# The zeroth MLP group's Relus pinned in ScalarE's order, and its sum operands spaced further apart

## The chip, the cores and the metric

The kernel runs on one core of one Trainium2 chip. The metric is the device time of one execution in microseconds (us). TensorE is named PE in the profile, VectorE DVE, ScalarE ACT, GpSimd POOL and SyncE SP.

## The reference

A hybrid decoder layer on 512 tokens of width 2048: attention heads and a recurrence side by side, then an MLP with a squared Relu. Only the MLP's entry matters here.

```python
h = rmsnorm(x, g_norm_mlp[l]).astype(jnp.float32) * (1.0 + sc2) + sh2
hid = jnp.square(jax.nn.relu(jnp.einsum('bsd,df->bsf', h, w_mlp_in[l].astype(jnp.float32))))
y = jnp.einsum('bsf,fd->bsd', hid, w_mlp_out[l].astype(jnp.float32))
x = (x.astype(jnp.float32) + gt2 * y).astype(x.dtype)
...
return rmsnorm(x, g_norm_final)
```

`w_mlp_in` is 2048 x 8192, `w_mlp_out` 8192 x 2048, all in float32.

## The kernel before

Every float32 operand of a matmul is split into a high part (a rounding copy on ScalarE) and a low part (the difference, on VectorE), and a product is three matmuls: high by high, high by low and low by high. `split` (L124) does it for activations, with its two instructions at L126 and, through `low`, at L122; `operands` (L1053) does it for weights. L122 is thus the line of all low parts, whatever their tile.

The 8192 hidden columns are done in 16 groups of 512. The tokens are cut in two halves of 256, A and B.

The zeroth group (g = 0) is a plain product, `half_product` (L991), in 16 steps of k for half A and 16 for half B (lines 259, 262 and 263 on PE, weight copies at L244). Each half writes two banks of PSUM: A a `z` and an `mm`, B an `o` and an `mm`. There are eight banks: three `z`, four `mm` and one `o`. `relu_half` (L977) empties a half's two banks with two Relus on ScalarE (L981). `keep_parts` (L928) then squares them, splits them and writes parts and sums to DRAM through POOL's queue (lines 932 to 949).

Groups 1 to 15 are products after Strassen and Winograd, in `strassen` (L1083): per group eight steps j, in each step seven products of two halves and three matmuls (lines 1102 to 1104), which is 42 matmuls of 256 columns. The seven products sum up in seven banks, taken in turn; group 1 has `z` `z` `z` `mm` `mm` `mm` `mm`, group 2 begins with `o`. Group 1 takes j from 7 down to 0, the others from 0 up. For each step `operands` loads 512 KB of weights on SP's queue (L1058), forms the weight sums on VectorE (lines 1060, 1067, 1068), and splits raw weights (a ScalarE copy of 768 columns at L1066, into tiles `w3`) and sums (one of 1024 columns at L1072, into tiles `w4`/`w5`). There are six `w3` tiles and five of 1024 columns, and one set takes two of each.

The activation sums are made once, in `sums` (L907): for each j from 7 to 0, four VectorE operations of 256 columns (L912 to L915), and two splits of 512 columns each (L126, L122). Group 1 needs the sums of j at its step j.

The order on each engine is fixed before the run. A scheduler walks a modelled time line, and on each engine takes the ready instruction with the highest priority. Priority is the place in program order; `tc.high_priority(offset=n)` moves the enclosed instructions n places forward. `tc.keep_in_program_order(ins)` adds an order-only edge: on its engine `ins` comes behind the instruction that was traced just before it. SETW (200) is the offset of the operands, SETE (330) that of what empties the banks at a group's end.

Work beside the products is traced by generators in lanes (`bg`). After each step `tick()` takes 1.0 off the lane's wait, and while the wait is not above zero the lane's next piece is traced; a piece yields the wait that it adds. `norm3`, `prep_b` and `sums` are queued before half A, `keep_parts(0)` after half B. By these numbers `sums` traces j = 7 at the third step of half B (16 steps), 6 at the sixth, 5 at the ninth, 4 at the twelfth, and 3, 2, 1, 0 at the 13th to 16th. `acts_in` (L1123) makes sure that a j is traced before its use.

Of the kernel before, what the change touches and what calls it, by code (L numbers as in the profile page):

```python
# [12 lines left out]
AF = mybir.ActivationFunctionType  # L13
# [51 lines left out]
def hybrid_layer_kernel(  # L65
# [32 lines left out]
    def T(tag, dt=F32, cols=None):  # L98
        return new(next(split_tag) if tag == "w4" else tag, dt, cols)
# [13 lines left out]
    act = nc.scalar.activation  # L113
# [7 lines left out]
    def low(out, full, high):  # L121
        tt(out=out, in0=full, in1=f32(high), op=ALU.subtract)  # L122

    def split(full, tag):  # L124
        h = T(tag, F32R)
        act(h, full, AF.Copy)  # L126
        lo = T(tag, F32R)
        low(lo, full, h)
        return h, lo
# [311 lines left out]
    for o in range(8):  # L441
        t = T("a")
# [275 lines left out]
    def mix(k, src, gcol, r):  # L718
        stt(out=src, in0=src, scalar=gcol, in1=r, op0=ALU.mult, op1=ALU.mult)
        mixed[k] = split(src, "a")  # L720
# [138 lines left out]

    KP = NK // 2
    NG = DFF // 512
    HT = 256
# [2 lines left out]
    raw_h, raw_l, fin, fin2, half2, other, sums_ = {}, {}, {}, {}, {}, {}, {}  # L867
# [10 lines left out]
    def prep_a(r2):  # L878

        for k in PAIRED:  # L880
            j, c = k % KP, k // KP
            if c == 0:
# [9 lines left out]
    def prep_b(r2):  # L892

        for k in BACK:
            j, c = k % KP, k // KP
            if c == 0:
# [10 lines left out]
    def sums():  # L907

        for j in range(KP)[::-1]:
            f1, f2 = fin[j], fin2[j]  # L910
            s12, s34 = T("n"), T("n")
            tt(out=s12[:, q_(0)], in0=f2[:, q_(0)], in1=f2[:, q_(1)], op=ALU.subtract)  # L912
            tt(out=s34[:, q_(0)], in0=f1[:, q_(0)], in1=f2[:, q_(0)], op=ALU.subtract)
            tt(out=s12[:, q_(1)], in0=s12[:, q_(0)], in1=f1[:, q_(0)], op=ALU.subtract)
            tt(out=s34[:, q_(1)], in0=f1[:, q_(1)], in1=s12[:, q_(1)], op=ALU.add)  # L915
            sums_[j] = [split(t, "a") for t in (s12, s34)]
            yield 3.0 if j > 4 else 1.0

    def norm3(tok, prep, ptag):
        yield 5.0  # L920
# [7 lines left out]
    def keep_parts(g, r11, r12, r22, r21, dt=1.0):  # L928

        for n, r in enumerate((r11, r12, r22, r21)):  # L930
            if g:
                act(r, r, AF.Relu)
            act(r, r, AF.Square)
            if n < 3 or p21D[g]:
                for i, t in enumerate(split(r, "a")):
                    dst = (
                        partD[g].rearrange("p (b f i t) -> p b f i t", b=2, f=3, i=2)[:, :, n, i, :] if n < 3
                        else p21D[g].rearrange("p (b i t) -> p b i t", b=2, i=2)[:, :, i, :]
                    )
                    nc.gpsimd.dma_start(dst, f32(t).rearrange("p (b t) -> p b t", b=2))  # L940
            yield dt
        dst = sumD[g].rearrange("p (b n t) -> p b n t", b=2, n=4)
        s1, s2 = T("a"), T("a")
        for n, (out, i0, i1, op) in enumerate((
            (s1, r21, r22, ALU.subtract), (s2, s1, r11, ALU.subtract), (r11, r11, r21, ALU.subtract),
            (r12, r12, s2, ALU.add),
        )):
            tt(out=out, in0=i0, in1=i1, op=op)
            nc.gpsimd.dma_start(dst[:, :, n, :], out.rearrange("p (b t) -> p b t", b=2))
            yield dt  # L950
# [26 lines left out]
    def relu_half(bs):  # L977

        rs = T("a"), T("a")
        for r, b in zip(rs, bs):  # L980
            act(r, b, AF.Relu)  # L981
        return rs


    PAIRED = [k for j in range(KP) for k in (j, j + KP)]
    BACK = [k for j in range(KP)[::-1] for k in (j, j + KP)]

# [20 lines left out]
    def h2_half(tok):  # L1008
        def of(k):
            j, c = k % KP, k // KP  # L1010
            if tok.start == 0:
                return raw_h[j][:, q_(c)], raw_l[j][:, q_(c)]
            side = half2 if c else other
            while j not in side:
                assert bg.next()
            return side[j][:, q_(0)], side[j][:, q_(1)]
# [22 lines left out]
    for k in range(12, NK):  # L1039
        nc.gpsimd.dma_start(x1D[k], x1[k])  # L1040
    b2 = [bank("z"), bank("mm")]
    bg.add(norm3(B, prep_b, "z"), sums())
    held = {}
    half_product(b2, in_src(0), h2_half(A), PAIRED, held, dict(zip(PAIRED[6:], ["w3"] * 3 + ["ts"] * 2 + ["w4"] * 5)))
    r11, r12 = relu_half(b2)
    b2 = [bank("o"), bank("mm")]
    half_product(b2, in_src(0), h2_half(B), BACK, held)
    r21, r22 = relu_half(b2)
    bg.add(keep_parts(0, r11, r12, r22, r21, 0.7))

    SETW, SETE = 200, 330

    def operands(src):  # L1053

# [28 lines left out]
    def strassen(src, acts, after=None, pre=None, before=None, js=range(8)):  # L1083

        bs = [bank(next(turn)) for _ in PRODUCTS]
        if pre:
            n, ts = pre
            with tc.high_priority(offset=SETE):
                for b, t in zip(bs, ts):
                    act(b, t, AF.Copy)  # L1090
                for b, t in zip(bs[5:], load_pre(n, (5, 6), nc.scalar)):
                    act(b, t, AF.Copy)
        if before:
            loaded[0] = before()
        for j in js:
            w, a = operands(src(j)), acts(j)
            for b, (an, wn) in zip(bs, PRODUCTS):
                (ah, al), (wh, wl) = a[an], w[wn]
                for i in range(2):
                    out, st = b[:, q_(i)], j == js[0] and i == 0 and not pre  # L1100
                    kw = dict(skip_group_check=True)
                    mm(out, wh[:, blk(i)], ah, start=st, stop=False, **kw)  # L1102
                    mm(out, wh[:, blk(i)], al, start=False, stop=False, **kw)  # L1103
                    mm(out, wl[:, blk(i)], ah, start=False, stop=j == js[-1], **kw)  # L1104
            if after:
                after(j)
            tick()
        return bs
# [108 lines left out]
    for g in range(1, NG):  # L1217
# [3 lines left out]
        bs = strassen(lambda j: w_pair[j][:, :, g * 512 : (g + 1) * 512], acts_in, last, js=range(KP)[:: -1 if g == 1 else 1])  # L1221
        with tc.high_priority(offset=SETE):
            r = [T("a") for _ in range(4)]
            q11, q12, q22, q21 = combine(bs, *r)

            rs = q12, q11, q21, q22
# [30 lines left out]
    for i, (n, ps) in enumerate(parts):  # L1257
# [15 lines left out]
        bs = strassen(src, acts_out, after, nxt, before, ps)  # L1273
        nxt = loaded[0]
        if n not in left:
# [11 lines left out]
            with tc.high_priority(offset=SETW):  # L1287
                for k, tok, q in quarters(n, *qs):
                    t = x2[k][:, tok]
# [5 lines left out]
        else:  # L1295
            with tc.high_priority(offset=SETE):
                for j, b in enumerate(bs):
                    t = T("a")
# [14 lines left out]
    for p in final:  # L1313
        t = T("a", F32R)
# [51 lines left out]
    def part(o, i):  # L1366

        if o == 0 and i == 3:
            for k in range(11, NK):
                sums(A, k)  # L1370
            bg.add(norm4(A))
        if o > 0 and i == 3:
            sums(B, 10 + o)
# [95 lines left out]
```

## Time and profile before

| | us |
|---|---|
| median of 3 runs | 1995.27 |
| lowest, highest run | 1991.86, 1996.58 |
| the profiled execution | 1994.49 |
| its span in the profile | 1992.7 |
| PE busy | 1941.9 |
| DVE busy | 1760.6 |
| ACT busy | 1074.6 |
| POOL busy | 193.6 |

The rows shown below are of the profiled execution; their first number is the start in us from the beginning of the span, the second the duration. In brackets stands how long the engine was idle before the instruction, and what ended that. A PE row's duration is modelled and overlaps the next; the distance of starts tells the pace. DVE and ACT rows overlap a little too.

### The profile page before, as it was taken

What the parts mean: (1) busy time and instruction counts of PE and PEld (TensorE: products, weight loads), DVE (VectorE), ACT (ScalarE), POOL (GpSimd) and SP (SyncE); (2) the same over time, 40 slices, a digit from 0 to 9 for tenths busy, and PEclk for the clock granted to TensorE, in tenths of its full rate; (3) what the DMA queues carried; (4) which work ended last, traced back from release to release, by engine and by line L of the source; (5) the groups of instructions that cost most, each with busy time, mean ns of one, the idle gap of its engine ahead of it and who ended that gap; (6) DMA issues with size and microseconds to landing.
All of it is one profiled execution on the core that took longest, in us unless ns stands there. A gap on an engine that the chain in (4) does not pass through costs nothing. (4 is left out here: it accounts for less than half of the span.)

```text
span 1992.7 us, 37203 instructions
## 1 busy us (share of the span) xinstructions
PE 1941.9 (97%) x14148; PEld 1815.3 (91%) x14148; DVE 1760.6 (88%) x2979; ACT 1074.6 (54%) x1580; POOL 193.6 (10%) x307
## 2 busy tenths in 40 slices
PE   8999999999999998999999999999999999999997
PEld 6787887788888998999999999999999999999996
DVE  8998776988998599999999999999879779879996
ACT  5443564786433385555555555556445555556552
POOL 0000000000000000112111211200110210211100
PEclk9999999999999999999999999999999999999998
DMA  9896655556779544766666665755567668679653
GB/s 368 304 340 198 212 163 185 179 163 218 226 251 365 170 134 129 239 194 213 221 196 203 226 197 190 232 173 210 185 241 262 238 249 278 220 253 341 225 197 112
DMA packets 205238, 443.51 MB, mean 223 GB/s; under 512 B 20481, under 2 KB 42113, under 8 KB 205058
## 3 DMA queue, kind: packets, MB, share of 16 engines
q1 hardware_dynamic: 176338, 356.58, 54.2%
q0 software_dynamic: 23680, 77.61, 10.5%
q10 hardware_dynamic: 5040, 6.93, 1.0%
q8 instruction: 111, 1.82, 0.4%
q14 instruction: 69, 0.57, 0.1%
HBM read 376.30 MB, written 64.75 MB: 221 GB/s over the span
## 5 line engine op out<-in xcount | busy, mean ns | idle before, releaser
L1102 PE MATMUL ps_mm<-a,w 128*128 128x256 f32 x1696 | 469.1, 277 | 3.0 <-DVE a L1114 1.2
L1104 PE MATMUL ps_mm<-a,w 128*128 128x256 f32 x1696 | 469.2, 277 | 0.4 <-DVE w L122 0.3
L1103 PE MATMUL ps_mm<-a,w 128*128 128x256 f32 x1696 | 469.1, 277 | 0.4 <-DVE a L122 0.3
L1072 ACT ACTIVATE w<-ts 128x1024 fp32r<-128x1024 f32 x244 | 258.4, 1059 | 273.1 <-DVE ts L1068 241.5
L1104 PE MATMUL ps_z<-a,w 128*128 128x256 f32 x1304 | 362.0, 278 | 6.9 <-DVE w L122 6.8
L1102 PE MATMUL ps_z<-a,w 128*128 128x256 f32 x1304 | 362.2, 278 | 3.4 <-DVE a L1118 1.6
L1103 PE MATMUL ps_z<-a,w 128*128 128x256 f32 x1304 | 361.4, 277 | 0.1
L122 DVE TENSOR_TENSOR w<-ts,w 128x1024 fp32r<-128x1024 f32 x244 | 297.8, 1221 | 55.4 <-PE ps_mm L1103 20.4
L1102 PEld LDWEIGHTS ps_mm<-a,w 128*128 128x128 f32 x1696 | 318.4, 188 | 4.3 <-issue 2.5
L1104 PEld LDWEIGHTS ps_mm<-a,w 128*128 128x128 f32 x1696 | 318.7, 188 | 1.1 <-DVE w L122 1.0
L1103 PEld LDWEIGHTS ps_mm<-a,w 128*128 128x128 f32 x1696 | 318.7, 188 | 0.8 <-DVE a L122 0.8
L122 DVE TENSOR_TENSOR w<-raw,w 128x768 fp32r<-128x768 f32 (+1 forms) x296 | 267.5, 905 | 37.8 <-ACT w L244 24.0
L1066 ACT ACTIVATE w<-raw 128x768 fp32r<-128x768 f32 x244 | 204.5, 839 | 174.8 <-issue 80.5
L1104 PEld LDWEIGHTS ps_z<-a,w 128*128 128x128 f32 x1304 | 245.6, 189 | 8.2 <-DVE w L122 8.1
L1102 PEld LDWEIGHTS ps_z<-a,w 128*128 128x128 f32 x1304 | 245.8, 188 | 4.9 <-issue 2.1
L1103 PEld LDWEIGHTS ps_z<-a,w 128*128 128x128 f32 x1304 | 245.7, 188 | 0.6 <-DVE a L122 0.6
L244 ACT ACTIVATE wh<-wr 128x512 fp32r<-128x512 f32 (+1 forms) x184 | 113.2, 618 | 142.4 <-PE ps_mm L262 61.8
L1060 DVE TENSOR_TENSOR ts<-raw 128x512 f32<-128x512 f32 x244 | 166.8, 684 | 14.2 <-DMA raw<-in_w_mlp_out_dram 13.4
L259 PE MATMUL ps_mm<-a,wh 128*128 128x512 f32 x448 | 176.8, 395 | 2.6 <-DVE a L460 1.0
L263 PE MATMUL ps_mm<-a,wl 128*128 128x512 f32 x448 | 175.0, 391 | 1.5 <-DVE wl L122 1.3
L262 PE MATMUL ps_mm<-a,wh 128*128 128x512 f32 x448 | 174.9, 390 | 0.0
L211 DVE SCALAR_TENSOR_TENSOR x<-x,cb 128x1024 f32<-128x1024 f32 x108 | 131.2, 1218 | 23.4 <-DMA x<-in_w_adaT_dram 23.3
(336 smaller groups left out, 4007.7 us busy)
## 6 DMA issues: line engine op xcount, KB each, us to landing
raw<-in_w_mlp_out_dram SPq DMA_DIRECT2D x124, 512.0 KB, 4.6
raw<-in_w_mlp_in_dram SPq DMA_DIRECT2D x120, 512.0 KB, 3.8
x<-in_w_adaT_dram SPq DMA_DIRECT2D x108, 512.0 KB, 5.6
wr<-in_w_in_dram SPq DMA_DIRECT2D x160, 256.0 KB, 3.4
tt<-in_w_adaT_dram SPq DMA_DIRECT2D x52, 512.0 KB, 6.2
part<-a POOLq DMA_DIRECT2D x84, 256.0 KB, 3.9
a<-part SPq DMA_DIRECT2D x84, 256.0 KB, 6.3
prod<-a POOLq DMA_DIRECT2D x63, 256.0 KB, 5.8
```

The costliest lines, as they stand in the source:

```text
L122: tt(out=out, in0=full, in1=f32(high), op=ALU.subtract)
L211: ins = stt(out=t, in0=t, scalar=1.0, in1=cb[q_], op0=ALU.mult, op1=ALU.mult, accum_out=self.ga[:, q_ : q_ + 1],)
L244: act(h[:, :n], r[:, :n], AF.Copy)
L259: first = mm(out, wh, ah, start=start, stop=False, **kw)
L262: mm(out, wh, al, start=False, stop=False, **kw)
L263: mm(out, wl, ah, start=False, stop=stop, **kw)
L1060: tt(out=t[:, : 2 * HT].rearrange("p (a b) -> p a b", a=2), in0=r[:, HT : 3 * HT].rearrange("p (a b) -> p a b", a=2), in1=r[:, q_(0)].unsq ...
L1066: act(h, r[:, HT:], AF.Copy)
L1072: act(h, t, AF.Copy)
L1102: mm(out, wh[:, blk(i)], ah, start=st, stop=False, **kw)
L1103: mm(out, wh[:, blk(i)], al, start=False, stop=False, **kw)
L1104: mm(out, wl[:, blk(i)], ah, start=False, stop=j == js[-1], **kw)
```

## The change

`sums` yields 3.0 for j above 3 (before: above 4), 2.0 for j of 3 and 2, and 1.0 for 1 and 0. By the ticks, j = 7 to 4 stay in their steps of half B, 3 goes to the 15th, and 2, 1 and 0 are traced after the first, third and fourth step of group 1. The ScalarE copies of the splits for j = 2, 1, 0 are pinned behind the ScalarE instruction traced just before each. The Relus of both halves get priority SETE and the same pin, and the `mm` bank comes first in each pair. SETW and SETE are defined earlier, with the same values.

```diff
-    def split(full, tag):
+    def split(full, tag, late=False):
         h = T(tag, F32R)
-        act(h, full, AF.Copy)
+        ins = act(h, full, AF.Copy)
+        if late:
+            tc.keep_in_program_order(ins)
         lo = T(tag, F32R)
         low(lo, full, h)
         return h, lo
...
+    SETW, SETE = 200, 330
...
-            sums_[j] = [split(t, "a") for t in (s12, s34)]
-            yield 3.0 if j > 4 else 1.0
+            sums_[j] = [split(t, "a", late=j < 3) for t in (s12, s34)]
+            yield 3.0 if j > 3 else 2.0 if j > 1 else 1.0
...
     def relu_half(bs):
 
         rs = T("a"), T("a")
-        for r, b in zip(rs, bs):
-            act(r, b, AF.Relu)
+        with tc.high_priority(offset=SETE):
+            for r, b in reversed(list(zip(rs, bs))):
+                tc.keep_in_program_order(act(r, b, AF.Relu))
         return rs
...
-    SETW, SETE = 200, 330
-
     def operands(src):
```

## The prediction

> **What bounds the kernel now.** I read the page's totals first, then a table of busy time by stage, then the waits of that stage, then the instructions in order of time on TensorE, ScalarE and VectorE.
>
> ```profile
> PE 1941.9 (97%) x14148; PEld 1815.3 (91%) x14148; DVE 1760.6 (88%) x2979; ACT 1074.6 (54%) x1580; POOL 193.6 (10%) x307
> ```
>
> TensorE is the bound on average, so time can come only from places where it does not run. The table shows such a place where the MLP begins (columns: busy us of PE, PEld, DVE, ACT, POOL, granted clock, DMA share, GB/s).
>
> ```profile
> 768.00:781.00 13.00, 7.21 (x55) 6.82 (x54) 13.00 (x28) 7.89 (x14) 0.00 (x0) 0.87 0.20 63
> 781.00:793.00 12.00, 12.00 (x93) 11.98 (x91) 8.91 (x14) 5.70 (x10) 2.88 (x5) 0.86 0.27 81
> ...
> 754.00:805.00 51.00, 44.23 (x351) 43.03 (x351) 47.03 (x83) 27.13 (x40) 5.42 (x8) 0.93 0.48 158
> 805.00:843.00 38.00, 37.29 (x325) 36.89 (x324) 36.89 (x60) 21.91 (x29) 6.80 (x10) 1.00 0.67 205
> ...
> 1400.00:1500.00 100.00, 100.00 (x885) 100.00 (x884) 80.64 (x122) 47.20 (x58) 10.22 (x19) 1.00 0.64 223
> ```
>
> From 768 to 781 us VectorE is busy all the time and TensorE only 7.21 of 13 us; just after it, VectorE has room (8.91 of 12). So work for VectorE is bunched. A matmul costs 100 us / 885 = 0.113 us where nothing disturbs (1400 to 1500). Of the waits between 754 and 805 us (total, times, longest) this one carries TensorE's loss:
>
> ```profile
> PE ps_z L1104 <- DVE w L122: 6.2, 4, 4.2
> ```
>
> TensorE waits for a low half of weights from VectorE. In order of time:
>
> ```profile
> 758.89 0.28 PE L1102 MATMUL ps_z<-a,w 128*128 128x256 f32 x1
> ...
> 770.72 0.28 PE L1103 MATMUL ps_z<-a,w 128*128 128x256 f32 x1
> 772.61 0.39 PE L1104 MATMUL ps_z<-a,w 128*128 128x256 f32 x1 [1.61 <-DVE w L122]
> 772.83 0.28 PE L1102 MATMUL ps_z<-a,w 128*128 128x256 f32 x1
> 772.95 0.28 PE L1103 MATMUL ps_z<-a,w 128*128 128x256 f32 x1
> ...
> 779.58 0.58 PE L1104 MATMUL ps_z<-a,w 128*128 128x256 f32 x1 [4.18 <-DVE w L122]
> 779.96 0.42 PE L1102 MATMUL ps_z<-a,w 128*128 128x256 f32 x1
> 780.17 0.42 PE L1103 MATMUL ps_z<-a,w 128*128 128x256 f32 x1
> ...
> 784.43 0.28 PE L1103 MATMUL ps_z<-a,w 128*128 128x256 f32 x1
> 784.55 0.28 PE L1104 MATMUL ps_z<-a,w 128*128 128x256 f32 x1
> 784.67 0.28 PE L1102 MATMUL ps_mm<-a,w 128*128 128x256 f32 x1
> ...
> 807.53 0.28 PE L1102 MATMUL ps_o<-a,w 128*128 128x256 f32 x1
> ```
>
> Group 1 runs from 758.89, right behind the zeroth group's second half, to 807.53, where group 2 opens with its bank `o`: 48.64 us. It has 8 x 7 x 6 = 336 matmuls, at 0.113 that is 38.0 us. So 10.6 us are lost here. Two terms are large: the 4.18 us wait, and the stretch behind it, 779.96 to 784.43, where starts lie 0.21 apart instead of 0.113: 4.47 us of which 4.47 x (1 - 0.113/0.21) = 2.1 are loss.
>
> Why does it wait? ScalarE:
>
> ```profile
> 742.38 0.51 ACT L902 ACTIVATE a<-n,mods 128x256 f32<-128x256 f32 x1
> 742.78 0.59 ACT L981 ACTIVATE a<-ps_z 128x512 f32<-128x512 f32 x1
> ...
> 755.20 0.61 ACT L244 ACTIVATE w<-raw 128x512 fp32r<-128x512 f32 x1
> ...
> 757.07 1.06 ACT L1072 ACTIVATE w<-ts 128x1024 fp32r<-128x1024 f32 x1 [0.52 <-DVE ts L1068]
> ...
> 760.87 0.85 ACT L1066 ACTIVATE w<-raw 128x768 fp32r<-128x768 f32 x1 [2.74 <-DMA raw<-in_w_mlp_in_dram]
> ...
> 764.90 1.06 ACT L1072 ACTIVATE w<-ts 128x1024 fp32r<-128x1024 f32 x1 [1.71 <-DVE ts L1068]
> ...
> 780.48 0.57 ACT L981 ACTIVATE a<-ps_o 128x512 f32<-128x512 f32 x1
> 780.96 0.58 ACT L981 ACTIVATE a<-ps_mm 128x512 f32<-128x512 f32 x1
> ...
> 786.35 1.06 ACT L1072 ACTIVATE w<-ts 128x1024 fp32r<-128x1024 f32 x1 [3.77 <-PE ps_mm L1104]
> ```
>
> Half B's two Relus (L981, the last pair) have their input at about 759.1 (the last matmul of half B starts just before 758.89 and runs 0.28) and run at 780.5 and 781.0. Nothing but their place in ScalarE's queue holds them: it idles 2.74 us right then. Until then the second one's bank `mm` is full, and it is the fourth `mm` bank that group 1 needs for its seventh product. So that product's matmuls of j = 7 to 4 come only from 784.67 on, and the weight tiles they read stay taken: each operand set takes two of the five 1024-column tiles, so the third set (copied at 764.90) finds no tile for its low half.
>
> VectorE shows that, and gives the prices:
>
> ```profile
> 754.39 0.69 DVE L1060 TENSOR_TENSOR ts<-raw 128x512 f32<-128x512 f32 x1 [0.69 <-DMA raw<-in_w_mlp_in_dram]
> ...
> 757.48 0.69 DVE L1060 TENSOR_TENSOR ts<-raw 128x512 f32<-128x512 f32 x1
> 758.08 0.95 DVE L122 TENSOR_TENSOR w<-raw,w 128x768 fp32r<-128x768 f32 x1
> 758.95 1.22 DVE L122 TENSOR_TENSOR w<-ts,w 128x1024 fp32r<-128x1024 f32 x1
> 760.08 0.42 DVE L1067 TENSOR_TENSOR ts<-ts,raw 128x256 f32<-128x256 f32 x1
> 760.42 0.69 DVE L122 TENSOR_TENSOR a<-n,a 128x512 fp32r<-128x512 f32 x1
> 761.02 0.42 DVE L1068 TENSOR_TENSOR ts<-ts,raw 128x256 f32<-128x256 f32 x1
> 761.36 0.69 DVE L1060 TENSOR_TENSOR ts<-raw 128x512 f32<-128x512 f32 x1
> ...
> 786.23 2.43 DVE L122 TENSOR_TENSOR w<-ts,w 128x1024 fp32r<-128x1024 f32 x2 [2.83 <-PE ps_mm L1103]
> ...
> 800.44 1.22 DVE L122 TENSOR_TENSOR w<-ts,w 128x1024 fp32r<-128x1024 f32 x1
> ```
>
> That low half is written at 786.23, after 2.83 us of waiting for the seventh product; the circle is closed there. Start to start, an operand set costs 0.60 + 0.87 + 1.13 + 0.34 + 0.34 = 3.28 us of VectorE, and one j of the sums four 256-column operations and two 512-column low halves, 4 x 0.34 + 2 x 0.60 = 2.56.
>
> **The change part by part.** No instruction, DMA or byte is added or removed; orders change.
>
> Relus of half A: the pin puts them behind the prep copies traced before them. They run right behind one already (742.38, 742.78), without a gap: 0.
>
> Relus of half B, the `mm` bank first, priority raised: the pin's last predecessor is the weight copy at 755.20 (L244). They can go when TensorE ends half B, at 759.1, into the 2.74 us gap before 760.87; two take about 1.05 (780.48 to 781.43 is 0.48 each, start to start). The seventh product of j = 7 is due 36 matmuls behind 758.89, at 763.0, so it finds its bank, and the low half of the third set no longer waits for 786.
>
> Spacing: j = 7, 6, 5, 4 of the sums keep their steps, j = 3 comes three steps behind j = 4 instead of one, at the 15th of half B's 16 steps; j = 2, 1, 0 land behind the first, third and fourth steps of group 1, each before its use (sixth, seventh, eighth). So their VectorE work, 2.56 each, no longer stands in front of the fourth operand set. Queue order for the split copies of these three: behind the 1024-column copies of j = 7, 5 and 4. At j = 7 and 5 that was so already (copies at 757.07 and 764.90, sums later); for j = 0 it is new, and costs nothing if that copy comes by 780, since its sum is used last.
>
> How far can group 1 shrink? VectorE is then the limit. From 754.39 it owes: 8 operand sets, 26.2; sums of j = 3 to 0, 10.2; what is left of j = 5 and 4, about 1.5 and 2.2; one weight low half, 0.6. Sum 40.8, so it could be through at 795.2. In the profile its last operand of group 1 (800.44) ends at 801.7: the difference is the 2.83, small handshakes, and some 2.7 us of the zeroth group's own splits and of group 2's operands in between. Behind its last operand TensorE needs at least four products of six matmuls, 2.7 us; in the profile it took 807.5 - 801.7 = 5.8.
> - Best end: 795.2 + 2.7 = 797.9, a gain of 9.6 us. (TensorE's own floor is 758.9 + 38.0 = 796.9.)
> - Poor end: 795.2 + 3.3 (handshakes and foreign work) + 5.8 = 804.3, a gain of 3.2.
> - I take the middle, 6.4, since order is set by costs that I cannot see.
>
> In both ends the remaining waits are spread over eight steps of at most 2.6 us each, so I leave out the slow stretch. The nearest rows: behind the 1.61 us wait the starts are 0.12 apart, behind the 4.18 us wait 0.21. The Trainium skill, page "TensorE: Matmul & The Clock Gate", section "What's actually happening", says that the clock falls to one half after an idle window of about 3.4 us and comes back after as long a busy one. Both rows agree with it; by its figure the slow stretch would cost about 1.7 us where the trace has 2.1.
>
> What is late next: the zeroth group's parts (L933, L126, L948) start four to five steps later in program order. Before, three splits and two sums of it, 5 x 0.60 = 3.0 us of VectorE, ran inside group 1. They now fall on group 2, where VectorE has 1.1 us free in 38. They feed only DMAs of POOL's queue that are read back much later, so they may slide on; bounds 0 and 3.0. I take 0.5, near the low end, since no operand set waits behind them by priority. SP's loads of raw weights move forward with the buffers; the DMA share there is 0.48, so they have room: 0.
>
> Sum: 6.4 - 0.5 = 5.9 us. The profiled execution took 1994.49 (span 1992.7 and 1.8 around it), 0.8 less than the median of 1995.27; from the median the forecast is 1989.4, and behind group 1 nothing else is forecast to move.
>
> **The rivals.**
> - VectorE's time is conserved. It is 92% busy from 754 to 805 and 97% in group 2, so pushed-off work may come back as waits later. Then only its 2.83 us wait is won: 1995.3 - 2.8 = 1992.5. For it: the 36.89 of 38. Against: TensorE runs 37.29 of those 38 us.
> - The pinned Relu blocks ScalarE. If it is placed right behind the copy at 755.20, it stands at about 755.7 and waits for 759.1; the copies of j = 6 and j = 7 behind it come 3.4 us later, and VectorE with them: 1989.4 + 3.4 = 1992.8. Against: it is issued only when the schedule holds its bank for complete. The Trainium skill, same page, section "Architectural detail", calls ScalarE's queue a strict FIFO; the 3.77 us in which ScalarE runs nothing ahead of the waiting copy at 786.35 agree.
> - The Relus do not move, and the order stays about as it is: 1995.3. Against: the idle gap above.
> - Slower: the late sums become what TensorE waits for. The place is the split copies of j = 2, 1, 0, pinned behind the 1024-column copies; if one of these waits for a weight tile as at 786.35 (3.77 us), the split and the low half on VectorE wait too. Three such waits are 11.3 us, with one slow stretch 13.4. It decides, that is it costs 4 us net, once they reach 5.9 + 4.0 = 9.9: 1995.3 - 5.9 + 13.4 = 2002.8. For it: five tiles for two per set. Against: the late use.
>
> **How the numbers follow.** 0.2% is 4.0 us, about what a measurement of this kernel can tell. The forecast (gain 3.2 to 9.6, less 0.5) has 0.72, of which 0.67 beyond 4.0; conserved time 0.12, same; blocked ScalarE 0.06, half faster, half same; no move 0.05, same; late sums 0.05, slower. Faster 0.70, same 0.25, slower 0.05. The forecast's own range is 1985.7 to 1992.5; with the two cases at 1992.5 and 1992.8 and their spread of some 1.5 the range is 1985.3 to 1994.2.
>
> **What would show it.** Right: L981 of banks `mm` and `o` near 760 instead of 780; group 1's seventh product in turn; no wait of L1104 over 3.4 us; granted clock 1.00 from 768 to 793; first `ps_o` of group 2 near 801; VectorE's wait at 783 gone. Wrong: L1102 or L1103 waiting for `a` of L122, ScalarE idle before L981, or group 2 and 3 longer than before by what group 1 won.

## The result, and the profile after

The change made the kernel slower: a median of 1999.68 us in 11 runs against 1995.27 us in 11 runs of the kernel before, ratio 1.0023 (95% interval 1.0014 to 1.0032). Forecast were 1989.4 us, a range that ended at 1994.2, and a chance of 0.05 for slower.

The profiled execution that came with these runs was a disturbed one of 6918.82 us in which the matmuls were slow; such executions count in the medians of this document but not in its ratios, which so need not be the quotients of the medians. The profile after is therefore read from the run `again`, which has the same instructions in the same order on each engine and the line numbers of the kernel before. That execution took 2000.34 us, with a span of 1998.6; before had a span of 1992.7.

First the table of busy time by stage, of `again`, for the stretches shown of before and the ones behind them (busy us of PE, PEld, DVE, ACT, POOL, granted clock, DMA share, GB/s):

```profile
768.00:781.00 13.00, 9.28 (x67) 9.08 (x67) 12.99 (x26) 8.53 (x14) 0.00 (x0) 0.87 0.14 42
781.00:793.00 12.00, 12.00 (x108) 12.00 (x107) 11.17 (x19) 5.75 (x8) 0.00 (x0) 1.00 0.44 132
...
806.00:820.00 14.00, 9.16 (x64) 8.92 (x64) 10.86 (x18) 5.80 (x9) 3.38 (x5) 0.76 0.59 218
754.00:805.00 51.00, 46.23 (x384) 45.30 (x382) 49.35 (x89) 28.71 (x41) 2.74 (x4) 0.97 0.47 145
805.00:843.00 38.00, 32.68 (x269) 32.22 (x269) 33.81 (x58) 19.25 (x26) 10.17 (x15) 0.91 0.69 232
```

The reader compares the last two rows with those of before. From 754 to 805 us 384 matmuls run where 351 ran: the aimed-at place did gain. From 805 to 843 us only 269 run where 325 ran: a new hole, and the row of 806 to 820 us shows where it is, with TensorE busy 9.16 of 14 us and a granted clock of 0.76. Before, little was lost there:

```profile
806.00:820.00 14.00, 13.29 (x114) 12.89 (x114) 13.96 (x22) 9.59 (x15) 2.03 (x3) 1.00 0.51 157
```

TensorE's waits between 754 and 850 us in `again` (total, times, longest) name both places:

```profile
PE ps_mm L1102 <- ACT a L981: 3.7, 1, 3.7
PE ps_z L1102 <- ACT a L1113: 3.7, 1, 3.7
PE ps_o L1104 <- DVE w L122: 1.1, 1, 1.1
```

The waits of L1104 behind L122, weights' low halves, that led this list before (6.8 us in this window, 6.2 of them up to 805 us) have shrunk to 1.4 (1.1 at `ps_o`, 0.3 at `ps_z`). In their place TensorE waits once for a Relu of half B (L981), and once for L1113, the ScalarE copy that begins the combination of group 1's banks and so frees the first bank for group 2. ScalarE in order of time:

```profile
766.37 0.63 ACT L126 ACTIVATE a<-n 128x512 fp32r<-128x512 f32 x1 [0.47 <-DVE n L914]
...
771.06 1.30 ACT L126 ACTIVATE a<-n 128x512 fp32r<-128x512 f32 x2 [2.38 <-DVE n L914]
772.26 0.83 ACT L1066 ACTIVATE w<-raw 128x768 fp32r<-128x768 f32 x1
773.00 0.58 ACT L981 ACTIVATE a<-ps_mm 128x512 f32<-128x512 f32 x1
773.47 0.59 ACT L981 ACTIVATE a<-ps_o 128x512 f32<-128x512 f32 x1
...
804.13 0.63 ACT L126 ACTIVATE a<-a 128x512 fp32r<-128x512 f32 x1 [2.44 <-DMA part<-a]
804.67 0.83 ACT L1066 ACTIVATE w<-raw 128x768 fp32r<-128x768 f32 x1
805.41 1.04 ACT L1072 ACTIVATE w<-ts 128x1024 fp32r<-128x1024 f32 x1
810.96 0.60 ACT L1113 ACTIVATE a<-ps_z 128x512 f32<-128x512 f32 x1 [4.51 <-DMA part<-a]
```

Two things are to be seen. The Relus came forward from 780.5 to 773.0, not to 759: sum copies (L126) that wait for VectorE still stand ahead of them. And the copy L1113, which ran at 804.49 before, runs at 810.96, because its *output* tile is still being read by a DMA that writes a part of the zeroth group to DRAM (`part<-a`); ScalarE idles 4.51 us for that, and 2.44 us for another tile just before. In the kernel before the copy does not wait:

```profile
804.49 0.57 ACT L1113 ACTIVATE a<-ps_z 128x512 f32<-128x512 f32 x1
```

POOL's queue shows how late these DMAs are issued, first in `again`:

```profile
799.62 0.70 POOL L940 DMA_DIRECT2D part<-a  x1 [85.00 <-ACT a L126]
...
808.67 0.68 POOL L940 DMA_DIRECT2D part<-a  x1 [2.94 <-DVE a L122]
```

and then in the kernel before:

```profile
782.35 0.70 POOL L940 DMA_DIRECT2D part<-a  x1 [67.79 <-ACT a L126]
...
794.19 0.68 POOL L940 DMA_DIRECT2D part<-a  x1 [0.67 <-DVE a L122]
```

The zeroth group's six parts went out between 782 and 794 us, well ahead of group 1's combination; now they go out between 800 and 809 us, across it. TensorE in `again`:

```profile
773.62 0.39 PE L1102 MATMUL ps_mm<-a,w 128*128 128x256 f32 x1 [3.73 <-ACT a L981]
...
774.33 0.41 PE L1103 MATMUL ps_mm<-a,w 128*128 128x256 f32 x1
774.54 0.41 PE L1104 MATMUL ps_mm<-a,w 128*128 128x256 f32 x1
...
803.54 0.28 PE L1102 MATMUL ps_o<-a,w 128*128 128x256 f32 x1
...
811.61 0.58 PE L1102 MATMUL ps_z<-a,w 128*128 128x256 f32 x1 [3.72 <-ACT a L1113]
811.99 0.41 PE L1103 MATMUL ps_z<-a,w 128*128 128x256 f32 x1
812.21 0.41 PE L1104 MATMUL ps_z<-a,w 128*128 128x256 f32 x1
```

Group 2 opens at 803.54 (807.53 before). Eighteen matmuls later it needs the `z` bank, waits 3.72 us, and then runs at 0.21 us from start to start, half pace, as it did behind the 3.73 us wait at 773.62. The Trainium skill, page "TensorE: Matmul & The Clock Gate", section "What's actually happening", gives an idle window of about 3.4 us for the fall to half clock; both rows agree.

The fixed order on TensorE has changed as well. In the kernel before, only six `ps_o` matmuls of group 2 stand ahead of its first `ps_z` one:

```profile
808.21 0.28 PE L1102 MATMUL ps_z<-a,w 128*128 128x256 f32 x1
```

In `again` it is eighteen, those of three steps, so TensorE comes sooner to the operands of the later steps and waits for them, 0.48 us at 805.55 and 1.12 us at 807.17. An estimate from these rows: the three waits of this stage make 5.3 us, and from 811.61 to 814.98 fifteen matmuls take 3.4 us where 15 x 0.113 = 1.7 would do; less the one wait of 0.64 us that the kernel before has in this stage, that is 6.4 us.

Four marks cut the span into stages: the first matmul of group 1, the first `ps_o` of group 2, and the L1113 of groups 2 and 15. All profiled executions, in us:

| kernel | group 1 to `ps_o` | `ps_o` to combination of 2 | 2 to 15 | 15 to the end | first part issued |
|---|---|---|---|---|---|
| before | 48.6 | 37.7 | 507.4 | 640.1 | 782.4 |
| before_again | 48.0 | 37.8 | 505.7 | 640.1 | |
| again (the change) | 44.4 | 44.3 | 505.7 | 645.0 | 799.6 |
| again_2 (the change) | 45.1 | 44.5 | 506.8 | 644.4 | |
| relus | 47.8 | 38.6 | 509.9 | 641.7 | |
| sums | 45.6 | 44.0 | 505.0 | 646.6 | |
| c_in_n | 44.3 | 43.9 | 506.2 | 644.2 | |
| parts_late | 45.9 | 44.7 | 505.6 | 644.6 | 786.0 |
| parts_early | 42.5 | 38.4 | 509.8 | 643.2 | 780.2 |
| parts_early_2 | 43.8 | 38.5 | 507.2 | 641.7 | |
| early_parts | 42.0 | 41.7 | 505.4 | 643.1 | |
| early4_parts | 43.4 | 41.3 | 509.1 | 641.0 | |
| lane_alone | 48.5 | 39.2 | 506.5 | 640.1 | 782.6 |

From before to `again`: -4.2, +6.6, -1.7, +4.9 and +0.3 ahead of group 1, together +5.9, the difference of the two spans. So there are two losses to explain, one in group 2 and one behind group 15, and a gain that is smaller than forecast.

The mark at the first `ps_o` is the end of group 1 only where all 336 matmuls of group 1 run ahead of it. That is so in the first eight rows and in `lane_alone`. In `parts_early` and `parts_early_2` 22 of them run behind it, in `early_parts` and `early4_parts` 24. Counted by matmuls, 336 have begun after 45.1, 46.6, 48.3 and 47.9 us in these four, against 48.6 and 48.0 in the two executions of the kernel before.

### The profile page after: what moved, and what is told of

Read it like the earlier page. It is cut to its first block, busy times and chain, and to the rows that moved or that the text cites. A ratio compares the mean times of both kernels' runs of the same rounds, so it can differ in the third digit from the quotient of the medians.

```text
span 6917.1 us, 37211 instructions
## 1 busy us (share of the span) xinstructions
PE 6898.7 (100%) x14148; PEld 5852.2 (85%) x14148; DVE 1799.5 (26%) x2979; ACT 1105.9 (16%) x1580; POOL 192.7 (3%) x307
## 4 chain that ended last, share of the span: by engine, by line
PE 100%; DVE 0%; ACT 0%; DMA 0%; issue 0%; DVEq 0%
PE ps_mm L1105 10%; PE ps_mm L1104 10%; PE ps_mm L1106 10%; PE ps_z L1105 8%; PE ps_z L1106 8%; PE ps_z L1104 8%; PE ps_mm L261 7%; PE ps_mm L264 7%; PE ps_mm L265 7%; PE ps_z L261 3%; PE ps_z L264 3%; PE ps_z L265 3%; PE ps_o L1105 3%; PE ps_o L1104 2%; PE ps_o L1106 2%; PE ps_o L264 1%
## 5 line engine op out<-in xcount | busy, mean ns | idle before, releaser
L1105 PE MATMUL ps_mm<-a,w 128*128 128x256 f32 x1696 | 1176.4, 694 | 0.0
L1106 PE MATMUL ps_mm<-a,w 128*128 128x256 f32 x1696 | 1151.6, 679 | 0.0
L1104 PE MATMUL ps_mm<-a,w 128*128 128x256 f32 x1696 | 1151.1, 679 | 0.0
L1106 PEld LDWEIGHTS ps_mm<-a,w 128*128 128x128 f32 x1696 | 1028.6, 607 | 0.0
L1105 PEld LDWEIGHTS ps_mm<-a,w 128*128 128x128 f32 x1696 | 1004.6, 592 | 0.0
L1104 PEld LDWEIGHTS ps_mm<-a,w 128*128 128x128 f32 x1696 | 1003.5, 592 | 0.0
L122 DVE TENSOR_TENSOR w<-ts,w 128x1024 fp32r<-128x1024 f32 x244 | 298.8, 1224 | 2667.3 <-PE ps_mm L1105 1495.9
L1105 PE MATMUL ps_z<-a,w 128*128 128x256 f32 x1304 | 902.8, 692 | 0.0
L1106 PE MATMUL ps_z<-a,w 128*128 128x256 f32 x1304 | 884.6, 679 | 0.0
L1104 PE MATMUL ps_z<-a,w 128*128 128x256 f32 x1304 | 884.0, 678 | 0.0
L1106 PEld LDWEIGHTS ps_z<-a,w 128*128 128x128 f32 x1304 | 789.4, 606 | 0.0
L1104 PEld LDWEIGHTS ps_z<-a,w 128*128 128x128 f32 x1304 | 772.7, 593 | 0.0
L1105 PEld LDWEIGHTS ps_z<-a,w 128*128 128x128 f32 x1304 | 771.5, 592 | 0.0
L261 PE MATMUL ps_mm<-a,wh 128*128 128x512 f32 x448 | 492.0, 1099 | 0.0
L264 PE MATMUL ps_mm<-a,wh 128*128 128x512 f32 x448 | 491.4, 1097 | 0.0
L265 PE MATMUL ps_mm<-a,wl 128*128 128x512 f32 x448 | 487.7, 1090 | 0.0
L122 DVE TENSOR_TENSOR wl<-wr,wh 128x512 fp32r<-128x512 f32 (+1 forms) x184 | 126.4, 687 | 1341.7 <-ACT wh L246 1008.9
L122 DVE TENSOR_TENSOR w<-raw,w 128x768 fp32r<-128x768 f32 (+1 forms) x296 | 267.5, 905 | 316.3 <-ACT w L246 171.0
L264 PEld LDWEIGHTS ps_mm<-a,wh 128*128 128x128 f32 x448 | 195.7, 437 | 169.4 <-issue 169.2
L261 PEld LDWEIGHTS ps_mm<-a,wh 128*128 128x128 f32 x448 | 191.4, 427 | 172.7 <-issue 170.1
```

The source lines that it names most:

```text
L261: first = mm(out, wh, ah, start=start, stop=False, **kw)
L264: mm(out, wh, al, start=False, stop=False, **kw)
L265: mm(out, wl, ah, start=False, stop=stop, **kw)
```

## The experiments

Edits are against the kernel before, or against the change where that is said. `later` is the kernel's short name for `tc.keep_in_program_order`.

**again, relus and sums: the change, and its two halves.** `again` is the change itself. `relus` has only the Relus' half:

```diff
-        for r, b in zip(rs, bs):
-            act(r, b, AF.Relu)
+        with tc.high_priority(offset=SETE):
+            for r, b in reversed(list(zip(rs, bs))): later(act(r, b, AF.Relu))
```

and `sums` only the other:

```diff
-            sums_[j] = [split(t, "a") for t in (s12, s34)]
-            yield 3.0 if j > 4 else 1.0
+            sums_[j] = [split(t, "a", late=j < 3) for t in (s12, s34)]
+            yield 3.0 if j > 3 else 2.0 if j > 1 else 1.0
```

Expected of `again`: 

> The changed kernel once more, its lines laid out so that their numbers are those of the kernel before; the instructions and their order are the same. Two theories of where some 4 us went. (A) Group 1 itself is no shorter: the Relus of half B still come late in ScalarE's order, and the late sums are waited for: first ps_z of group 1 to first ps_o of group 2 takes 52 to 55 us against 48.6, the rest of the span as before within 2 us. (B) The forecast is right for group 1, 41 to 45 us, and it is lost behind it: groups 2 to 15 together take 8 to 12 us more than before. Time 1998 to 2001 us in both.

Expected of `relus`: 

> The Relus' half alone: priority, pin and the mm bank first; the sums are spaced as before and their copies not pinned. In ScalarE's order the two Relus of half B still stand behind all twelve split copies of the sums and seven copies of raw weights, as before; only their own order is turned. Theory (A'), that the Relus are held by the place at which the schedule's model has half B end, and not by priority: L981 at 780 to 782 us, time within 0.2% of before. My forecast's theory, that priority moves them: L981 near 760 and 1990 us or less.

Expected of `sums`: 

> The sums' half alone: the spacing and the three pinned split copies; the Relus as before. Under theory (A'), all of the change's effect is in the spacing: time like the whole change, 1998 to 2001 us, and the same group times within 1 us. If the Relus matter by themselves, it is 3 us or more off the whole change.

Measured beside one another: `again` 2001.82 against 1997.74, ratio 1.0020 (1.0007 to 1.0032); `relus` 1996.79, ratio 0.9994 (0.9981 to 1.0008); `sums` 2002.36, ratio 1.0025 (1.0009 to 1.0041). Of the two theories, (B) has group 1 right, but of its 8 to 12 us in groups 2 to 15 there are 4.9 by the table, and another 4.9 lie behind group 15. The whole effect is in the sums' half; its spacing and its three pins were not tried apart. ScalarE in `relus` shows why the other half does nothing:

```profile
782.23 0.63 ACT L126 ACTIVATE a<-n 128x512 fp32r<-128x512 f32 x1 [0.57 <-DVE n L915]
782.77 0.58 ACT L981 ACTIVATE a<-ps_mm 128x512 f32<-128x512 f32 x1
783.25 0.59 ACT L981 ACTIVATE a<-ps_o 128x512 f32<-128x512 f32 x1
```

With priority and pin the Relus run at 782.8, behind the last of the sum copies as before. In `sums`, with neither, they run early, in the same place of ScalarE's order as in `again`, only with `o` ahead of `mm`:

```profile
776.35 0.58 ACT L981 ACTIVATE a<-ps_o 128x512 f32<-128x512 f32 x1
```

So it is the sums that stand ahead of the Relus that place them, not priority or pin. The priority takes effect among instructions that are ready on the modelled time line. That the model ends half B later than the chip does is an inference from the order, not something that a trace shows.

**parts_early and c_in_n: the late parts, or the tile?** Both are the change plus one line. `parts_early` traces the zeroth group's parts in a lane that is empty at that point, beside the sums and not behind them:

```diff
-    bg.add(keep_parts(0, r11, r12, r22, r21, 0.7))
+    bgl.add(keep_parts(0, r11, r12, r22, r21, 0.7))
```

`c_in_n` leaves them late and gives group 1's L1113 a tile of another pool:

```diff
-            r = [T("a") for _ in range(4)]
+            r = [T("n" if g == 1 and not i else "a") for i in range(4)]
```

Expected of `parts_early`: 

> The changed kernel with the zeroth group's keep_parts in a lane of its own, so that it is traced from half B's end on as before the change, not behind the late sums. Theory P: what the change lost is group 1's first bank copy (L1113), which waits 4.5 us for its output tile until a part of the zeroth group has been written to DRAM, and the slow stretch behind it. Then L1113 no longer waits for a part's DMA, the time from group 1's first matmul to group 2's L1113 falls from 88.7 to 84 to 86 us, and the kernel gains 3 to 4 us on the change. Rival Q: VectorE's time is what counts; the parts' work then falls into group 1 and the same sum is lost there: 87.5 us or more, time as the change.

Expected of `c_in_n`: 

> The changed kernel; only the tile that group 1's L1113 writes comes from the pool n (five tiles, also used by the late adaLN rows) instead of the full pool a. Theory P: L1113 of group 1 runs as soon as its bank is done, near 806 instead of 811; the wait of 3.7 us on TensorE and the slow stretch behind it are gone; group 1's first matmul to group 2's L1113 falls by 3 us or more, time 2 to 4 us under the change. Rival Q: the next operation of the combination waits for the same tile, and less than 1 us is won.

Measured, against 1995.24 of before: `parts_early` 1993.38 in 11 runs, ratio 0.9989 (0.9978 to 0.9999); `c_in_n` 2000.15 in 6 runs, ratio 1.0028 (1.0017 to 1.0040). TensorE's waits between 754 and 850 us in `parts_early` begin so, and nothing else there is over 0.4:

```profile
PE ps_mm L1102 <- ACT a L981: 3.7, 1, 3.7
```

The wait for L1113 is gone, the one for the Relu has stayed. From group 1's first matmul to group 2's combination it takes 80.9 us, less than the 84 to 86 that were expected. Group 2 in the table by stage of `parts_early` is whole again, 334 matmuls for the 269 of `again`:

```profile
805.00:843.00 38.00, 38.00 (x334) 37.77 (x333) 38.00 (x64) 21.22 (x28) 7.45 (x11) 1.00 0.70 217
```

In `c_in_n` L1113 runs at 800.59, but the wait goes one instruction on. First TensorE's wait, then VectorE in order of time:

```profile
PE ps_z L1102 <- DVE a L1114: 4.6, 1, 4.6
```

```profile
808.07 0.69 DVE L122 TENSOR_TENSOR a<-a,a 128x512 fp32r<-128x512 f32 x1 [1.45 <-DMA part<-a]
...
811.44 0.69 DVE L1114 TENSOR_TENSOR a<-ps_z,n 128x512 f32<-128x512 f32 x1 [0.28 <-DMA part<-a]
```

L1114, the next step of the same combination, needs an `a` tile too, and waits 0.28 us for the same DMAs. More of its delay lies ahead of it in VectorE's order: a low half of the parts (L122) waits 1.45 us for such a DMA at 808.07, and two of the parts' sums (L948) stand between. The expectation that freeing the first tile would help missed; the theory holds only in a wider form, "the late parts hold tiles and places in the queues".

**parts_late: the delay alone.** The kernel before, with the parts put off by four steps of the lane and nothing else:

```diff
     def keep_parts(g, r11, r12, r22, r21, dt=1.0):
-
+        if not g: yield 4.0
```

Expected: 

> The kernel before with one thing of the change alone: the zeroth group's keep_parts starts four ticks later, where the change puts it; Relus and sums as before. Theory P: its parts reach DRAM later, the tiles of pool a stay taken, and group 1's L1113 or the operation behind it waits for a part's DMA: group 1's first matmul to group 2's L1113 88 us or more against 86, and 2 to 4 us slower than before. Rival: with the sums early VectorE gets to the parts in time all the same; same time as before within 0.1%, no wait for a part's DMA.

Measured: 2004.20 against 1997.06, ratio 1.0032 (1.0021 to 1.0043). With no sum moved and no Relu touched, this gives a slowdown of at least that size (2 to 4 us were expected, and the medians differ by 7.1), in the same stages of the table: +7.0 in group 2 and +4.5 behind group 15 against before. It even shortens group 1, by 2.7, as the parts' VectorE work leaves it. The way is another, though. ScalarE in `parts_late`:

```profile
813.97 1.06 ACT L1072 ACTIVATE w<-ts 128x1024 fp32r<-128x1024 f32 x1 [4.16 <-DVE ts L1068]
814.93 0.58 ACT L1113 ACTIVATE a<-ps_z 128x512 f32<-128x512 f32 x1
```

Here L1113 stands behind a weight copy that waits for VectorE. From 754 to 835 us no engine waits for a part's DMA, so the expected wait for tiles missed. Of the parts' own late work only one sum (L948 at 809.31, 0.6 us) stands in VectorE's order ahead of what that copy waits for. What is as in `again` is the fixed order on TensorE: eighteen `ps_o` matmuls of group 2 ahead of the first `ps_z` one, with waits of 0.64 and 2.29 us for weights among them and 1.68 us for L1113 behind them. The parts' DMAs go out at 786.0 to 795.7 here, only 1.5 to 3.7 us later than before; the sums behind them (first L949 at 810.3, before 803.2) fall into group 2. So a delay of this lane alone is shown to be enough for a loss of this size in these stages, and without a wait for a part's DMA ahead of them; how the delay makes the scheduler choose this order is not shown. That the loss of the change itself comes from its late parts is shown by `parts_early`, which takes it away; that most of it goes through a tile rests on the 4.51 us that L1113 waits in `again`. That the two sizes agree may be chance.

**early_parts and early4_parts: the Relus all the way forward.** The change, with parts in the empty lane, and more sums traced inside group 1, their copies ordered behind the Relu itself (an order-only edge) in place of the pin:

```diff
-        ins = act(h, full, AF.Copy)
-        if late:
-            tc.keep_in_program_order(ins)
+        with tc.issue_after(relus[-1].ins) if late else ExitStack(): act(h, full, AF.Copy)
...
-            sums_[j] = [split(t, "a", late=j < 3) for t in (s12, s34)]
-            yield 3.0 if j > 3 else 2.0 if j > 1 else 1.0
+            sums_[j] = [split(t, "a", late=j < 6) for t in (s12, s34)]
+            yield 3.0 if j > 6 else 11.0 if j > 5 else 1.0
```

`early4_parts` has `late=j < 5` and 3.0, 8.0 and 1.0 for j above 5, of 5 and below.

Expected of `early_parts`: 

> What the forecast took for given is made true: the sums of j = 5 to 0 are traced in group 1 and their ScalarE copies are ordered behind the second Relu, so that in ScalarE's order the Relus of half B stand behind three raw copies and two 1024-column copies alone; keep_parts of the zeroth group as in parts_early. By the forecast's reasoning: L981 at 761 to 766 us, no wait of TensorE for a Relu over 1 us, group 1 in 39 to 43 us, time 3 to 6 us under the kernel before. Rival Q: VectorE is full from 724 us on and has all of the sums still to do, so group 1 takes 44 us or more whatever the Relus do, and the time is within 0.2% of before.

Expected of `early4_parts`: 

> As parts_early, but the sums of j = 4 to 0 are traced in group 1 (j = 5 stays in half B) and their copies are ordered behind the second Relu, so that the Relus stand behind three raw copies, two 1024-column copies and the sums of j = 7 to 5. parts_early still shows a wait of 3.7 us of TensorE for a Relu with a slow stretch behind it; early_parts shows none, but a wait for the late sums. If the two can be had apart: L981 at 763 to 767 us, no wait over 1.6 us in group 1, group 1's first matmul to group 2's L1113 77 to 80 us against 80.9 in parts_early, time 1990 to 1993 us. Rival Q (VectorE is full, what is won at one place is waited for at the next): 80 us or more, and the time within 1 us of parts_early.

Measured: `early_parts` 1994.25 against 1995.24, ratio 0.9994 (0.9982 to 1.0006); `early4_parts` 1995.31 against 1997.06, ratio 0.9994 (0.9979 to 1.0008). Neither beats `parts_early`. ScalarE in `early_parts` has the Relus where the prediction wanted them:

```profile
761.97 0.58 ACT L981 ACTIVATE a<-ps_mm 128x512 f32<-128x512 f32 x1
```

but TensorE now waits for the sums themselves, in `early_parts`

```profile
PE ps_z L1103 <- DVE a L122: 3.0, 1, 3.0
```

and in `early4_parts`:

```profile
PE ps_z L1102 <- ACT a L126: 2.8, 2, 2.5
```

The row of `early_parts` from 754 to 805 us says why:

```profile
754.00:805.00 51.00, 45.00 (x364) 43.34 (x363) 50.75 (x93) 27.65 (x40) 6.78 (x10) 0.97 0.50 163
```

VectorE is busy 50.75 of 51 us. Once the Relus are out of the way its own work is the bound of this stretch in `early_parts`; in `early4_parts` it is busy 48.35 of 51 us, and the bound is less plain. Group 1 is hardly shorter than in the kernel before in either, 48.3 and 47.9 us to its 336th matmul: its last step waits for the last of the sums and runs behind the first twelve matmuls of group 2, so the 42.0 and 43.4 in the table are the time to a mark and no gain.

**lane_alone: whose gain is parts_early's?** The kernel before with only the one line of `parts_early`.

Expected: 

> The kernel before, with nothing of the change, but the zeroth group's parts in a lane of their own, so that they are traced beside the sums of j = 3 to 0 and not behind them. It tells whether the gain of the run with both (0.9989) is the change's own gain, freed of the late parts, or the lane's. Theory (the gain is the change's): the parts were early already (first part's DMA at 782.4, long landed before group 1's combination at 804.5), so the lane alone brings nothing in group 1; with the parts' VectorE work, 3.0 us, moved ahead of the seventh product's operands it may even cost: first product of group 1 to that of group 2 48 to 51 us, to the second combination 85 to 89, ratio 0.9995 to 1.0010. Rival (the gain is the lane's: lane bg is through about eight ticks earlier, and what is queued behind the parts comes earlier too): to the second combination 81 to 84, ratio 0.9980 to 0.9992.

Measured: 1996.1 against 1997.25, ratio 1.0001 (0.9987 to 1.0016), and in TensorE's waits

```profile
PE ps_z L1104 <- DVE w L122: 6.7, 4, 4.2
```

stands as in the kernel before. The lane brings nothing by itself. The gain of `parts_early` is that of the change, once its late parts are taken away; its interval ends just below 1. Its two profiled executions show how little of it lasts. The 672 matmuls of groups 1 and 2 have begun after 83.6 and 85.1 us, against 88.1 and 87.8 in the kernel before, yet their spans of 1992.7 and 1993.4 us are no shorter than its 1992.7 and 1992.6. Why the rest is lost again was not tried.

**before_again, again_2 and parts_early_2: single executions, for what repeats.**

Expected of `before_again`: 

> The kernel before, unchanged, for a second profile: how far one execution's stages differ from another's with nothing changed. Group 1's first matmul to group 2's L1113 should come within 0.5 us of 86.3; if behind group 15's L1113 it differs from 640.1 by 2 to 5 us, then the 4.9 us that the changed kernel's profile lost there are not the change's.

Expected of `again_2`: 

> The changed kernel unchanged, for a second profile. Group 1 in 44 to 45 us, L1113 waiting 4 to 5 us for a part's DMA, group 1's first matmul to group 2's L1113 within 0.7 us of 88.7, and again 3 us or more lost against the kernel before between group 15's L1113 and 1425 us.

Expected of `parts_early_2`: 

> parts_early unchanged, for a second profile. Its first one has the clock at 0.83 from 1350 to 1360 us behind two waits of 1.2 us, where the two profiles of the kernel before have 1.00 behind the same two waits. If that is chance, it may be 1.00 here; if it belongs to the kernel, it is below 0.95 again. Group 1's first matmul to group 2's L1113 within 0.5 us of 80.9.

Measured once each: 1994.34, 2002.56 and 1995.08 us. The stages of the table repeat within 1.3 us in group 1 and 0.2 us from `ps_o` to the combination of group 2, so the loss there of 6.6 is far outside. The stage from group 2 to 15 varies by 1.7 us between two executions of the kernel before and by 2.6 between those of `parts_early`; its -1.7 in `again` is no result. The last stage repeats within 1.5 us.

**The second loss, behind group 15.** The stage takes 644.2 to 646.6 us in the five executions with late parts and 640.1 to 643.2 in the eight with parts in time. VectorE's waits between 1300 and 1450 us, first of `again`, then of before, then of `parts_late`:

```profile
DVE n L1203 <- DMA n<-in_w_adaT_dram: 3.4, 2, 3.1
```

```profile
DVE n L1203 <- DMA n<-in_w_adaT_dram: 0.3, 1, 0.3
```

```profile
DVE n L1203 <- DMA n<-in_w_adaT_dram: 3.6, 2, 3.3
```

The longest wait on this line is 2.4 to 3.8 us in all five with late parts, and at most 0.5 in all eight others. It sits here in `again`:

```profile
1336.57 0.68 DVE L1060 TENSOR_TENSOR ts<-raw 128x512 f32<-128x512 f32 x1
1340.38 0.69 DVE L1203 SCALAR_TENSOR_TENSOR n<-n,cb 128x512 f32<-128x512 f32 x1 [3.12 <-DMA n<-in_w_adaT_dram]
```

L1203 is part of an unrelated reduction that runs beside the groups; operands of the next product queue behind it. TensorE then waits in `again`

```profile
1357.46 0.39 PE L1102 MATMUL ps_mm<-a,w 128*128 128x256 f32 x1 [2.22 <-DVE a L1114]
```

where before the same wait is 1.16 us, and the clock from 1355 to 1360 us is 0.77 instead of 1.00. On SP's queue `again` issues ten reads of parts and sums (L1141, L1144) between 1329.14 and 1338.5 us, around the first weights of the next product; before, none of them comes until 1338.34, behind these weights. So the wait of L1203 goes with the late parts, without exception in thirteen executions. The time of the stage does so less sharply: 644.2 and 643.2 lie only 1.0 us apart, and `parts_early` and `early_parts` lose time there too, at a clock of 0.81 and 0.50 from 1350 to 1355 us. By which step a delay at 800 us changes the queues at 1330 us was not tried; that the lane of the later groups' parts never catches up (eight pieces of one step each in eight steps) is only argued.

## Why the prediction was wrong

- *What bounds the kernel, and the circle in group 1:* right as far as the change went. Group 1 shrank when the circle was loosened, by 4.2 and 3.5 us in two executions against 6.4 forecast (bounds 3.2 and 9.6), and by 3.5 and 2.0 with parts in time, counted by matmuls. With the Relus at 762 and six sums moved into group 1 (`early_parts`) it was 0.3 us: VectorE's work was then in the way.
- *"They can go when TensorE ends half B, at 759.1, into the 2.74 us gap":* failed. They went at 773.0. I read the gap in the trace as if ScalarE could take what is ready, but the order is fixed beforehand; `relus` shows that neither priority nor pin moves them. The seventh product did not find its bank: TensorE waited 3.73 us for it.
- *"I leave out the slow stretch":* failed with it. Half pace from 774.33 on followed that wait, as it did before.
- *"What is late next", the parts, bounds 0 and 3.0, taken 0.5:* the step that made the sign wrong. I counted their VectorE time and noted that their data is read much later. I did not count that they *hold tiles until their DMAs have landed*, and that group 1's combination writes into tiles of that pool. Measured: +6.6 in group 2, gone when the parts are early. The bound of 3.0 was a bound on work, not on a wait for space or on what a later lane does to the fixed order. The range left out even this bound: with 3.0 in place of 0.5 its slow end is 1995.27 - 3.2 + 3.0 = 1995.1, still short of the 1999.68 measured.
- *"Behind group 1 nothing else is forecast to move":* failed, by 4.9 us behind group 15.
- *The rivals:* the slower one had the right sign and the wrong place; in the change no split copy of j = 2, 1, 0 is waited for. Its mechanism does come, at 3.0 and 2.8 us, when six or five sums are late (`early_parts`, `early4_parts`). "VectorE's time is conserved" foresaw 2.8 us of gain; with the parts in time 1.9 are left (1995.24 to 1993.38). "The Relus do not move" had the mechanism of the Relus' half by itself (`relus`, 0.9994). "The pinned Relu blocks ScalarE" is not seen: in `again` the Relus run at 773.00 right behind a copy, without idle time.

## What to carry to other kernels

When work is put off, ask not only who reads its results but which buffers it holds until then, and who needs one next: a DMA that nobody waits for can still block an engine through its source tile. A gap in an engine's row is room only for an instruction that the fixed order allows there; see what stands ahead of it in the queue before giving it the gap. And if a change is split into lanes or queues, follow everything behind the delayed piece in the same lane: here one line that took the parts out of it turned a ratio of 1.0023 (1.0014 to 1.0032) into 0.9989 (0.9978 to 0.9999), the only one of the versions tried whose interval lies below 1, and that barely.

## What the runs showed of the hardware

Short waits close together can also halve the pace. In `parts_late` TensorE waits 0.64 us at 809.86 and 2.29 us at 812.65, and its starts lie 0.21 apart from 813.03 on:

```profile
812.65 0.58 PE L1104 MATMUL ps_o<-a,w 128*128 128x256 f32 x1 [2.29 <-DVE w L122]
813.03 0.41 PE L1102 MATMUL ps_o<-a,w 128*128 128x256 f32 x1
```

In `early4_parts` it waits 2.55 us at 789.95 and 0.43 at 790.89, and the clock from 792 to 797 us is 0.51. None of these waits is as long as the 3.72 and 3.73 us that went ahead of half pace in `again`.

A pair of waits of about 1.2 us, 2.6 us apart, around 1350 us left the clock at 1.00 in the kernel before and in `parts_early_2` but brought it to 0.81 (1350 to 1355 us) in `parts_early`, at the same place of the program. The Trainium skill, page "TensorE: Matmul & The Clock Gate", section "What's actually happening", calls the window free-running. That would let the same waits fall now inside one window and now across two; that this is the reason, no run here shows.
